# Joining an MLP's inner norm factor to its last norm, low parts on VectorE around it, and four split weight tiles kept between the token halves

## The chip, the core and the metric

The kernel runs on one core of a Trainium2 chip. The metric is the device time of one execution, in microseconds (us); less is better. The engines are called as in the profile: PE (TensorE's matmuls), PEld (its weight loads), DVE (VectorE), ACT (ScalarE), POOL (GpSimd) and SP (SyncE, which issues loads here).

## The reference

The whole program is a two-block network over 512 tokens of width 1024. The first block (a state-space mixer, a short convolution and an expert layer) is not touched. The part that matters is the end of the second block, after its two attentions `out_a` and `out_b`:

```python
def rmsnorm_2(x, g):
    y = x * rsqrt(mean(x * x, axis=-1) + EPS)      # EPS = 1e-6
    return y * g

merged = sigmoid(g_a) * (out_a @ w_o_a) + sigmoid(g_b) * (out_b @ w_o_b)
x = x + rmsnorm_2(merged @ w_out, post_norm_mix)
h2 = rmsnorm_2(x, pre_norm_mlp)
y = square(relu(h2 @ w_up)) @ w_down               # 1024 -> 4096 -> 1024
x = x + rmsnorm_2(y, post_norm_mlp)
```

All weights and activations are float32. The factor of the inner norm (`rsqrt(mean(x*x) + EPS)`, one number per token) is positive, so it can be taken through `relu` and through the matmuls, and out of the square as its own square.

## The kernel before

Everything is kept transposed: model width on the 128 partitions in 8 slices, tokens along the free dimension. A float32 product is made of three: each operand is split into a rounded high part and the low part that is left (`split`, L173 to 180: ScalarE rounds, another engine subtracts), and PE multiplies high by high, high by low and low by high (`mm3`, L201). One block is the product for one 128-wide slice of outputs: 8 slices of input times 3, that is 24 matmuls, over 512 tokens or over a half of 256.

Weights come through `weights` (L182): SyncE loads 512 KB into `wr` (3 buffers), ScalarE rounds it into `wh` (L176), and GpSimd, or VectorE where the call says so, subtracts it into `wl` (L177); `wh` and `wl` have 3 buffers each. In the stages below GpSimd makes the low parts, except for every second block of the last down-projection.

`block2` ends with these stages, in this order:

- The gated projections, 8 blocks of 512 tokens: products `po`, times the gates (`g`, L1223), added (`m`, L1225, on GpSimd), split into `m2h`, `m2l`.
- The output projection (`out_block`, L1233), run for tokens 0 to 255 and then for 256 to 511, 8 blocks (`psw`) each. ScalarE copies the result to `y` (the tile `oab`) and squares it, VectorE adds the squares up (`sqadd`, L1350).
- For each half `chain` (L1249): `norm` (L1239) takes row sums of the squares on PE (`ssqr`), a reciprocal root by 12 small VectorE instructions (`rsqrt`, names r3), a broadcast by PE (`prr`); then for each slice the scaling (L1255), the addition into the residual (L1256), the split into `d2h`, `d2l` with the MLP's gain (L179, L180), the square and its addition. At its end a second `norm` (r4) makes the factor of the inner norm, which ScalarE copies into `rb` (L1262).
- The up-projection, 4 quarters of 8 blocks (`up`, L1291; products `psup`). In the first quarter the first `nh` = 5 blocks run by halves, so that the first half's products cover the second half's chain, and the steps of the chains stand between the blocks. After each block `up_act` (L1285) takes `max(psup, 0) * rb` on VectorE, its square on ScalarE, and the split into `fh`, `fl`.
- The down-projection (`down`, L1314; products `psdn`), one quarter of the inner width behind each quarter of the up-projection; results are added up in `y`. The last quarter runs by halves again, with a norm (r5) and the final scaling and addition (`finish`, L1323) for each half. `finish` works on VectorE, with five of its eight additions on GpSimd.

Each engine works through its instructions in order. A list scheduler puts them in order from the program; `keep_in_program_order` holds the row sums and broadcasts at their place among PE's instructions. The order of the first quarter of the up-projection is written out by hand:

```python
for n, (j, tk) in enumerate([(j, tk) for tk in halves for j in range(nh)]
                            + [(j, slice(0, S)) for j in range(nh, 8)]):
    ready.append((f, j, tk, up_mm(q, j, n, tk)))
    if n == 0:
        next(first, None)
    if n in (0, 1, nh, nh + 1):
        next(second, None)
```

## Time and profile before

| | |
|---|---|
| median of 3 runs | 2861.68 us (2855.43 to 2865.1) |
| the profiled execution, its own time | 2858.98 us |
| its span, first to last instruction | 2857.1 us |
| granted TensorE clock over the span | 0.987 |
| PE busy | 2767.0 us, 97% |
| DVE / ACT / POOL busy | 1948.2 / 1095.3 / 854.9 us |

The page of the profile gives the busy sums for the whole span. The stages described above lie in its last 510 us, and times of events count from the span's start. Busy time of PE counts an instruction from start to modelled end, and consecutive matmuls overlap, so a block's duration is read from the distance of like events in neighbouring blocks or from a merged row of the chain of waits. The duration in a DVE row likewise overlaps a little with the next instruction; the distance of two starts is what it costs.

### The profile page before, as it was taken

The page shows a single profiled execution, that of the slowest core. Times are in us where ns is not written, and L with a number is a line of the kernel's source. Part 1 is how long each engine was busy: PE and PEld are TensorE (multiplying, and loading weights), DVE is VectorE, ACT ScalarE, POOL GpSimd, SP SyncE. Part 2 cuts the span into 40 slices and gives each one's busy share as a digit, 9 for nine tenths or more (in the row PEclk, how much of TensorE's full clock was granted, in tenths as well). Part 3 has the DMA queues.
Part 4 walks back from the last instruction along what each step waited for, and adds up shares of the span by engine and source line. Part 5 has one row for each costly group of instructions (what it writes and reads, how often), then busy time and mean ns, then how long its engine had stood idle before and what let it go on. Part 6 is the DMA issues. An engine that isn't in the chain of part 4 may idle for free. (4 is left out here: it accounts for less than half of the span.)

```text
span 2857.1 us, 40181 instructions
## 1 busy us (share of the span) xinstructions
PE 2767.0 (97%) x15502; PEld 2387.7 (84%) x15502; DVE 1948.2 (68%) x3687; ACT 1095.3 (38%) x1742; POOL 854.9 (30%) x464
## 2 busy tenths in 40 slices
PE   8999999999999999899999999999999999799997
PEld 7988888877888999899999998887787778788887
DVE  8433777775279997857887777888975655841236
ACT  4222433343233444444333333333345553443232
POOL 4444444444542002100322221222200016444443
PEclk9999999999999999999999999999999999899998
DMA  3222122223332668689988888999822225332223
GB/s 132 89 96 96 60 67 67 67 67 122 123 124 82 223 201 276 219 275 303 376 309 320 310 309 331 384 377 370 315 91 94 78 74 168 106 104 96 96 96 119
DMA packets 174736, 515.21 MB, mean 180 GB/s; under 512 B 14160, under 2 KB 75600, under 8 KB 158032
## 3 DMA queue, kind: packets, MB, share of 16 engines
q1 hardware_dynamic: 91328, 330.75, 33.8%
q0 software_dynamic: 18432, 134.23, 12.1%
q10 hardware_dynamic: 64784, 47.67, 5.2%
q8 instruction: 122, 2.00, 0.3%
q14 instruction: 70, 0.57, 0.1%
HBM read 462.97 MB, written 49.09 MB: 179 GB/s over the span
## 5 line engine op out<-in xcount | busy, mean ns | idle before, releaser
L176 ACT ACTIVATE wh<-wr 128x1024 fp32r<-128x1024 f32 (+1 forms) x525 | 553.8, 1055 | 1113.3 <-issue 239.5
L177 POOL TENSOR_TENSOR wl<-wr,wh 128x1024 fp32r<-128x1024 f32 x229 | 552.3, 2413 | 962.5 <-ACT wh L176 952.1
L851 POOL DMA_INDIRECT gb<-puv,idx x128 | 209.3, 1635 | 931.8 <-DVE gacc L860 779.3
L177 DVE TENSOR_TENSOR wl<-wr,wh 128x1024 fp32r<-128x1024 f32 (+1 forms) x296 | 359.6, 1216 | 153.7 <-ACT wh L176 150.3
L201 PE MATMUL psu<-u2h,wh 128*128 128x384 f32 x1024 | 348.9, 341 | 0.0
L201 PE MATMUL psu<-u2h,wl 128*128 128x384 f32 x1024 | 346.1, 338 | 1.4 <-DVE wl L177 1.4
L201 PE MATMUL psu<-u2l,wh 128*128 128x384 f32 x1024 | 345.1, 337 | 0.0
L201 PE MATMUL mmt<-uh,wh 128*128 128x264 f32 (+2 forms) x1016 | 328.8, 324 | 4.2 <-ACT uh L176 3.5
L201 PE MATMUL mmt<-ul,wh 128*128 128x264 f32 (+2 forms) x1016 | 329.0, 324 | 0.0
L201 PE MATMUL mmt<-uh,wl 128*128 128x264 f32 (+2 forms) x1016 | 326.5, 321 | 0.0
L1043 PE MATMUL acc<-wh,ch 128*128 128x512 f32 x768 | 305.9, 398 | 3.9 <-ACT ch L176 2.4
L1043 PE MATMUL acc<-wl,ch 128*128 128x512 f32 x768 | 305.7, 398 | 1.3 <-DVE wl L177 1.3
L1043 PE MATMUL acc<-wh,cl 128*128 128x512 f32 x768 | 305.4, 398 | 0.1
L201 PEld LDWEIGHTS mmt<-ul,wh 128*128 128x128 f32 x1016 | 192.3, 189 | 21.5 <-issue 10.0
L201 PEld LDWEIGHTS mmt<-uh,wh 128*128 128x128 f32 x1016 | 192.3, 189 | 19.0 <-ACT uh L176 3.7
L201 PEld LDWEIGHTS mmt<-uh,wl 128*128 128x128 f32 x1016 | 192.3, 189 | 15.0 <-issue 3.3
L201 PEld LDWEIGHTS psu<-u2h,wh 128*128 128x128 f32 x1024 | 194.7, 190 | 2.2
L201 PEld LDWEIGHTS psu<-u2l,wh 128*128 128x128 f32 x1024 | 194.3, 190 | 2.0
L201 PEld LDWEIGHTS psu<-u2h,wl 128*128 128x128 f32 x1024 | 193.7, 189 | 2.4 <-DVE wl L177 2.4
L1043 PEld LDWEIGHTS acc<-wl,ch 128*128 128x128 f32 x768 | 145.2, 189 | 38.5 <-DVE wl L177 3.5
L1043 PEld LDWEIGHTS acc<-wh,ch 128*128 128x128 f32 x768 | 145.3, 189 | 37.5 <-ACT ch L176 2.7
L1043 PEld LDWEIGHTS acc<-wh,cl 128*128 128x128 f32 x768 | 145.1, 189 | 33.1 <-DVE cl L177 0.4
(498 smaller groups left out, 5558.1 us busy)
## 6 DMA issues: line engine op xcount, KB each, us to landing
wr<-pu SPq DMA_DIRECT2D x128, 512.0 KB, 5.6
wr<-pv SPq DMA_DIRECT2D x128, 512.0 KB, 6.3
mg<-md SPq DMA_DIRECT2D x34, 768.0 KB, 10.4
md<-stg ACTq DMA_DIRECT2D x24, 1024.0 KB, 7.5
wr<-w_dn SPq DMA_DIRECT2D x40, 512.0 KB, 3.6
wr<-w_up SPq DMA_DIRECT2D x37, 512.0 KB, 3.7
actd<-at ACTq DMA_DIRECT2D x79, 192.0 KB, 3.8
ag<-actd SPq DMA_DIRECT2D x19, 768.0 KB, 6.8
```

The lines of the kernel that those rows point to most:

```text
L176: nc.scalar.activation(h, src, AF.Copy)
L177: (eng or nc.vector).tensor_tensor(l, src, h.bitcast(F32), op=OP.subtract)
L201: self.nc.tensor.matmul(ps, a[:, k], b, start=first and n == 0, stop=last and n == tot - 1)
L851: keep(nc.gpsimd.indirect_dma_start(out=rows[k][:NG], out_offset=None, in_=self.A["puv"], in_offset=bass.IndirectOffsetOnAxis(ap=idx[:NG, ...
L1043: self.nc.tensor.matmul(self.accs[i], a[:, t], b[:, d], start=e == self.e1 and n == 0, stop=e == self.e1 - 1 and n == 2)
```

## The change

The inner norm's factor is no longer applied between the up- and the down-projection. The MLP runs on the residual with only the gain, `relu` and square included, so its result is too large by the inverse square of the factor, per token; the last norm divides by its own root mean square anyway, and only its epsilon has to be corrected: with `e = mean(x*x) + EPS`, the last norm uses `EPS * e * e` in place of `EPS` (`eps4`). The sums for it are made during the second quarter's down-projection (`inner_norm`). `up_act` squares as `relu(psup)` on ScalarE and then `max(psup, 0)` times that on VectorE. In the first up-projection `nh` is 7.

Low parts of weights are made on VectorE in the gated projections, the output projection, the first quarter of the up-projection and the last of the down-projection, but on GpSimd for the blocks where `low` says so (a counter that leaves 1 when divided by 3). The addition of the gated projections goes to VectorE too.

`kept_weights` splits a weight tile into a slice of a pair of large tiles instead of the rotating `wh`, `wl`. In the output projection, the first quarter of the up-projection and the last of the down-projection, four of the blocks keep their split weights so from the first half to the second, which runs these four blocks first and loads nothing for them.

```diff
@@ -184,6 +184,15 @@
         self.nc.sync.dma_start(wr, ap)
         return self.wsplit(wr, kn, eng)
 
+    def kept_weights(self, ap, room, i, eng=None):
+        w = [t[:, 2 * i:2 * i + 2].rearrange("p a (b o) -> p (a b) o", o=128) for t in room]
+        if ap is not None:
+            wr = self.wraw.tile([128, 8, 128], F32, tag="wr", name="wr")
+            self.nc.sync.dma_start(wr, ap)
+            self.split(w[0], w[1], wr, eng=eng or self.nc.gpsimd)
+        return w
     def wsplit(self, wr, kn=8, eng=None):
         wh = self.whl.tile([128, kn, 128], F32R, tag="wh", name="wh")
         wl = self.whl.tile([128, kn, 128], F32R, tag="wl", name="wl")
@@ -222,12 +231,15 @@
             if keep and t == 0:
                 self.tc.keep_in_program_order(m)
 
-    def rsqrt(self, p, src, scale, tag, eps=True):
+    def rsqrt(self, p, src, scale, tag, eps=None):
 
         v = self.nc.vector
         shp = list(src.shape)
         x, y, a = [p.tile(shp, F32, tag=tag + n, name=tag + n) for n in ("x", "y", "a")]
-        v.tensor_scalar(x, src, scale, EPS, op0=OP.mult, op1=OP.add)
+        if eps is None:
+            v.tensor_scalar(x, src, scale, EPS, op0=OP.mult, op1=OP.add)
+        else:
+            v.scalar_tensor_tensor(x, src, scale, eps, op0=OP.mult, op1=OP.add)
         self.newton(x, y, a)
         return y
 
@@ -1215,14 +1227,14 @@
         for d in range(8):
             g2 = p.tile([128, 2, S], F32, name="g2")
             nc.sync.dma_start(g2, self.gd[d::8].rearrange("g p s -> p g s"))
-            wh, wl = self.weights(A["w_oab"][d])
+            wh, wl = self.weights(A["w_oab"][d], eng=v)
             for i, pp in ((0, self.mm2), (1, sp)):
                 ps = pp.tile([128, S], F32, tag=("mm", "s")[i], name="po%d" % i)
                 ks = slice(4 * i, 4 * i + 4)
                 self.mm3(ps, (wh[:, ks], wl[:, ks]), [(o[0][:, k], o[1][:, k]) for k in range(4 * i, 4 * i + 4)])
                 v.tensor_tensor(g2[:, i], g2[:, i], ps, op=OP.mult)
             t = p.tile([128, S], F32, name="m2")
-            nc.gpsimd.tensor_tensor(t, g2[:, 0], g2[:, 1], op=OP.add)
+            v.tensor_tensor(t, g2[:, 0], g2[:, 1], op=OP.add)
             self.split(m[0][:, d], m[1][:, d], t)
 
         y = oab
@@ -1230,17 +1242,24 @@
         H = S // 2
         halves = [slice(0, H), slice(H, S)]
 
+        low = lambda n: nc.gpsimd if n % 3 == 1 else v
         def out_block(d, tk):
             ps = (sp if d % 2 else self.mm2).tile([128, S], F32, tag="s" if d % 2 else "mm", name="psw2")[:, :H]
-            self.mm3_real(ps, self.weights(A["w_out"][d]), m, off=tk.start, n=H)
+            if d < 4:
+                w = self.weights(A["w_out"][d], eng=low(tk.start // H * d))
+            else:
+                w = self.kept_weights(None if tk.start else A["w_out"][d], kept, d - 4, v)
+            self.mm3_real(ps, w, m, off=tk.start, n=H)
             act.activation(y[:, d, tk], ps, AF.Copy)
-            self.sqadd(cn, y[:, d, tk], d, v, tk.start)
-
-        def norm(pool, tag, name, key):
+            self.sqadd(cn, y[:, d, tk], (d + 4) % 8 if tk.start else d, v, tk.start)
+        def norm(pool, tag, name, key, eps=None):
 
             ssq = pool.tile([128, 512], F32, tag=tag, name="ssq" + name)
             self.rowsum(ssq, self.sums[key], True, True, 2, keep=True)
-            r = self.rsqrt(cn, ssq[:, :2], 1.0 / D, name)
+            r = self.rsqrt(cn, ssq[:, :2], 1.0 / D, name, eps)
             yield
             pr = pool.tile([128, 512], F32, tag=tag, name="pr" + name)[:, :H]
             self.bcast(pr, r, 2, keep=True)
@@ -1255,66 +1274,82 @@
                 v.scalar_tensor_tensor(y[:, d, tk], y[:, d, tk], par("post_mix", d), pr, op0=OP.mult, op1=OP.mult)
                 v.tensor_tensor(x, x, y[:, d, tk], op=OP.add)
                 self.split(self.d[0][:, d, tk], self.d[1][:, d, tk], x, gain=par("pre_mlp", d))
-                self.sqadd(cn, x, d, v, "x")
             yield
-            n = norm(op_, "o", "r4", "x")
-            yield next(n)
-            act.activation(self.rb[:, tk], next(n), AF.Copy)
-
+        kept = [op2.tile([128, 8, S], F32R, name=n) for n in ("oh2", "ol2")]
         for d in range(8):
             out_block(d, halves[0])
         steps = chain(halves[0])
-        for d in range(8):
+        for n, d in enumerate((4, 5, 6, 7, 0, 1, 2, 3)):
             out_block(d, halves[1])
-            if d < 2:
+            if n < 2:
                 next(steps, None)
-        steps = (steps, chain(halves[1]))
+        steps = chain(halves[1])
         self.dump("x2", self.res)
         self.close("mgt2", "mg2", "ohl")
 
+        eps4 = cn.tile([128, 4], F32, name="eps4")
+        def inner_norm():
+            for d in range(8):
+                self.sqadd(p, self.res[:, d], d, v, "x")
+                yield
+            ssq = op_.tile([128, 512], F32, tag="o", name="ssqr4")
+            self.rowsum(ssq, self.sums["x"], True, True, 4, keep=True)
+            v.tensor_scalar(eps4, ssq[:, :4], 1.0 / D, EPS, op0=OP.mult, op1=OP.add)
+            v.scalar_tensor_tensor(eps4, eps4, EPS, eps4, op0=OP.mult, op1=OP.mult)
+            yield
         fp = self.open("ff", 2)
+        room = lambda: [fp.tile([128, 8, S], F32R, name=n) for n in ("fh", "fl")]
         p = self.open("fft", 2)
         fs = {}
+        nh = 7
+        kept = room()
 
         def up_mm(q, j, n, tk):
             ps = (sp if n % 2 and q == 0 else self.mm2).tile([128, S], F32, tag="s" if n % 2 and q == 0 else "mm",
                                                              name="psup")[:, tk]
-            self.mm3_real(ps, self.weights(A["w_up"][q * 8 + j]), self.d, off=tk.start, n=tk.stop - tk.start)
+            if q == 0 and nh - 4 <= j < nh:
+                w = self.kept_weights(None if tk.start else A["w_up"][j], kept, j - nh + 4, low(n))
+            else:
+                w = self.weights(A["w_up"][q * 8 + j], eng=None if q else low(n))
+            self.mm3_real(ps, w, self.d, off=tk.start, n=tk.stop - tk.start)
             return ps
 
         def up_act(f, j, tk, ps):
             r = p.tile([128, S], F32, name="r")[:, tk]
-            v.scalar_tensor_tensor(r, ps, 0.0, self.rb[:, tk], op0=OP.max, op1=OP.mult)
-            act.activation(r, r, AF.Square)
+            act.activation(r, ps, AF.Relu)
+            v.scalar_tensor_tensor(r, ps, 0.0, r, op0=OP.max, op1=OP.mult)
             self.split(f[0][:, j, tk], f[1][:, j, tk], r)
 
         def up(q):
-            f = fs[q] = [fp.tile([128, 8, S], F32R, name=n) for n in ("fh", "fl")]
+            f = fs[q] = room()
             if q:
                 for j in range(8):
                     up_act(f, j, slice(0, S), up_mm(q, j, j, slice(0, S)))
                 return
 
-            first, second = steps
-            next(first)
-            nh = 5
-            ready = []
-            for n, (j, tk) in enumerate([(j, tk) for tk in halves for j in range(nh)]
+            for n, (j, tk) in enumerate([(j, halves[0]) for j in range(nh)]
+                                        + [(j, halves[1]) for j in (*range(nh - 4, nh), *range(nh - 4))]
                                         + [(j, slice(0, S)) for j in range(nh, 8)]):
-                ready.append((f, j, tk, up_mm(q, j, n, tk)))
-                if n == 0:
-                    next(first, None)
-                if n in (0, 1, nh, nh + 1):
-                    next(second, None)
-                if n != nh:
-                    for x in ready:
-                        up_act(*x)
-                    ready = []
+                up_act(f, j, tk, up_mm(q, j, n, tk))
+                if n in (0, 1):
+                    next(steps, None)
 
         def down(f, q, d, tk):
             ps = sp.tile([128, S], F32, tag="s", name="psdn")[:, tk]
-            self.mm3_real(ps, self.weights(A["w_dn"][q, d], eng=v if q == 3 and d % 2 else None), f,
-                          off=tk.start, n=tk.stop - tk.start)
+            if q < 3 or d < 4:
+                w = self.weights(A["w_dn"][q, d], eng=v if q == 3 else None)
+            else:
+                w = self.kept_weights(None if tk.start else A["w_dn"][q, d], kept, d - 4, v)
+            self.mm3_real(ps, w, f, off=tk.start, n=tk.stop - tk.start)
             if q == 0:
                 act.activation(y[:, d, tk], ps, AF.Copy)
             else:
@@ -1328,22 +1363,29 @@
                 if d % 2:
                     nc.sync.dma_start(self.O[:, d - 1:d + 1, tk], y[:, d - 1:d + 1, tk])
 
+        inner = inner_norm()
         up(0)
         for q in range(3):
             up(q + 1)
             f = fs.pop(q)
             for d in range(8):
                 down(f, q, d, slice(0, S))
+                if q == 1:
+                    next(inner, None)
+            if q == 1:
+                next(inner)
         n, last = None, None
+        kept = room()
         for tk in halves:
-            for d in range(8):
+            for i in range(8):
+                d = (i + 4) % 8 if last else i
                 down(fs[3], 3, d, tk)
-                self.sqadd(cn, y[:, d, tk], d, v, tk.start)
-                if last and d == 0:
+                self.sqadd(cn, y[:, d, tk], i, v, tk.start)
+                if last and i == 0:
                     next(n)
-                if last and d == 1:
+                if last and i == 1:
                     finish(last, next(n))
-            n, last = norm(tp, "t", "r5", tk.start), tk
+            n, last = norm(tp, "t", "r5", tk.start, eps4[:, tk.start // 128:tk.start // 128 + 2]), tk
         next(n)
         finish(last, next(n))
```

## Rows read from the trace of the kernel before

**Rows 1.** The page, part 1: busy us, share of the span, instructions.

```profile
PE 2767.0 (97%) x15502; PEld 2387.7 (84%) x15502; DVE 1948.2 (68%) x3687; ACT 1095.3 (38%) x1742; POOL 854.9 (30%) x464
```

**Rows 2.** Five stretches: us; PE, PEld, DVE, ACT, POOL busy; clock; DMA.

```profile
2347.89:2453.50 105.61, 96.07 (x588) 86.09 (x586) 64.21 (x79) 44.24 (x75) 67.05 (x32) 0.97 0.49 157
2453.50:2525.55 72.05, 55.21 (x329) 50.42 (x329) 52.43 (x96) 32.69 (x62) 34.63 (x15) 0.83 0.33 107
2657.47:2702.27 44.80, 44.80 (x194) 36.07 (x193) 7.31 (x9) 9.65 (x11) 19.18 (x8) 1.00 0.30 96
2745.80:2842.97 97.17, 93.20 (x583) 83.73 (x581) 46.50 (x69) 29.83 (x39) 37.28 (x19) 0.98 0.36 117
2842.97:2857.10 14.13, 1.32 (x6) 0.89 (x6) 8.08 (x25) 0.42 (x1) 3.63 (x5) 0.57 0.22 74
```

**Rows 3.** PE's waits from 2347.89 to 2525.55: us, times, longest.

```profile
PE prr L246 <- DVE r4y L241: 11.1, 2, 8.1
PE psup L201 <- ACT d2h L179: 3.0, 2, 2.6
PE psw L201 <- ACT m2h L176: 2.7, 1, 2.7
PE psup L201 <- DVE d2l L180: 2.5, 2, 1.8
...
PE psw L201 <- DVE m2l L177: 1.7, 1, 1.7
...
PE po L201 <- DVE g L1223: 0.7, 1, 0.7
```

**Rows 4.** PE's waits from 2745.80 to 2857.10.

```profile
PE psdn L201 <- DVE oab L1321: 2.9, 1, 2.9
```

**Rows 5.** DVE in order of time: start us, us, instruction.

```profile
2442.55 0.86 DVE L1255 SCALAR_TENSOR_TENSOR oab<-oab,pt,prr 128x256 f32<-128x256 f32 x2
2443.34 0.41 DVE L1256 TENSOR_TENSOR res<-res,oab 128x256 f32<-128x256 f32 x1
2443.67 0.47 DVE L180 SCALAR_TENSOR_TENSOR d2l<-res,pt,d2h 128x256 fp32r<-128x256 f32 x1
2444.07 0.41 DVE L1358 TENSOR_TENSOR sq<-sq 128x256 f32<-128x256 f32 x1
...
2446.70 2.43 DVE L1256 TENSOR_TENSOR res<-res,oab 128x256 f32<-128x256 f32 x1
```

**Rows 6.** POOL's groups, 2347.89 to 2525.55: busy us, mean ns.

```profile
L177 POOL TENSOR_TENSOR wl<-wr,wh 128x1024 fp32r<-128x1024 f32 x38 | 92.1, 2431 | 88.8 <-ACT wh L176 88.7
```

**Rows 7.** The chain of waits: start us, us, what.

```profile
2401.12 13.19 PE psw L201 x96
...
2429.55 0.17 DVE r3a L239
...
2569.15 44.79 PE psdn L201 x192
2613.94 43.53 PE psup L201 x192
...
2829.83 13.15 PE psdn L201 x96
```

**Rows 8.** DVE in order of time, last down-projection.

```profile
2793.48 0.42 DVE L1321 TENSOR_TENSOR oab<-oab,psdn 128x256 f32<-128x256 f32 x1 [2.17 <-PE psdn L201]
...
2796.33 0.42 DVE L1321 TENSOR_TENSOR oab<-oab,psdn 128x256 f32<-128x256 f32 x1 [0.60 <-PE psdn L201]
...
2800.34 1.21 DVE L177 TENSOR_TENSOR wl<-wr,wh 128x1024 fp32r<-128x1024 f32 x1
2801.47 0.41 DVE L1358 TENSOR_TENSOR sq<-sq 128x256 f32<-128x256 f32 x1
```

**Rows 9.** One stretch, only instructions on d2h: PE, PEld, DVE, ACT.

```profile
2474.00:2480.00 6.00, 6.00 (x34) 5.17 (x34) 3.28 (x3) 1.50 (x3) 1.00 0.25 87
```

**Rows 10.** ACT in order of time, one weight tile's rounding.

```profile
2475.99 1.04 ACT L176 ACTIVATE wh<-wr 128x1024 fp32r<-128x1024 f32 x1
```

## The prediction

> **What bounds the kernel now.** I read the engine line of the page first [rows 1]. PE is busy for 97% of the span, so outside a few holes only fewer or faster matmuls could help, and the change removes none: whatever it gains must come out of holes. Then I cut the stages that the diff touches into stretches [rows 2]: A, the gated projections and the output projection; B, the first quarter of the MLP's up-projection; one ordinary down-projection for comparison; C, the last down-projections; and the tail after the last matmul. The comparison stretch has PE busy all 44.80 us at granted clock 1.00. A lacks 9.5 us of PE work, B lacks 16.8 us, C lacks 4.0 us, and the clock is below 1.00 in all three, at 0.83 in B. So each hole is paid for twice: while PE stands still, and afterwards at the lower of its two levels (1.2 instead of 2.4 GHz).
>
> The size of that second payment: a half block (24 matmuls over 256 tokens) takes 2.85 us at full clock, the distance between the two evictions at 2793.48 and 2796.33 [rows 8]. After the holes at the start of the output projection four half blocks took 13.19 us, and after the hole in the last stage 13.15 us [rows 7], where four times 2.85 is 11.4: about 1.8 us lost behind a hole.
>
> The waits say which work comes late. In A and B [rows 3] the largest is the broadcast of the inner norm's factor (r4), 11.1 us in two pieces; then the rounded input of the up-projection's second half (d2h and d2l, 5.5 us), then and the end of the merged input (m2h, m2l, 4.4 us). In C it is an eviction behind the final scaling, 2.9 us [rows 4]. What makes VectorE late there is seen in its own order of time [rows 5]: an addition into the residual takes 0.33 us (2443.34 to the next start), and the same addition at 2446.70 takes 2.43, which is the length of a low part on POOL (2431 ns, 38 of them in A and B, [rows 6]). VectorE stands until POOL's instruction is over.
>
> **The change part by part.** I compare each stretch with what its matmuls need without a hole. A full block is 43.53/8 = 5.44 us in an up-projection and 44.79/8 = 5.60 in a down-projection [rows 7], which I also take for a gated projection (512 columns too). The two PE steps of a norm, row sums and broadcast, are estimated at 1.0 us together: two of the one and one of the other cost what the holes around them leave, and the busy shares do not resolve more.
>
> *The inner norm leaves the front.* Both r4 chains (row sums, 12 small VectorE steps, broadcast) go from B: 11.1 us of waits and 2.0 us of PE steps. VectorE also loses 16 additions of squares there. The eight squares and additions that come instead, over 512 tokens, fall into the second down-projection, where VectorE is busy 7.31 and ScalarE 9.65 of 44.80 us [rows 2]; eight additions of 0.66 (twice the width of the 0.33), or 2.4 each behind POOL, still fit under PE. If that cover were gone they would cost 5.3 us. Not hidden are the four row-sum matmuls, some 0.6 us, which wait for the last addition: between 0 and 3 us (one eviction plus one blocked addition); I take 0.5, because the residual is ready long before. The corrected epsilon is one small instruction at each end norm where there was one already: nothing.
>
> *Relu on ScalarE, then a product on VectorE.* The same number of instructions as the product and the square now, in the other order; the accumulator is held by two steps instead of one. A half block's accumulators rotate over four buffers and a full block's over two, so there are at least 5.4 us for about 1.5. Nothing, while ScalarE has idle time; and the matmuls no longer wait through full buffers for the factor.
>
> *Low parts to VectorE.* One costs 1.13 us there (2800.34 to 2801.47, [rows 8]) against 2.43 on POOL. In A and B four stay on POOL (output block 1 of the second half, and n = 1, 4 and 13 in the up-projection); in C none. The sum for VectorE over output projection and first up-projection: 16 additions of squares at 0.33, 16 slices of the residual chain at 0.39 + 0.33 + 0.40 [rows 5], some 19 low parts at 1.13, 15 evictions and splits at 0.42 + 0.33 [rows 5, 8], 22 small steps at 0.17 [rows 7]: 60 us against 93 us of PE. The last merged slice no longer queues behind a low part on POOL, nor its m2l behind the next one; its addition, rounding and low part, three steps of some 0.65, run beside the 21 matmuls that do not need it (2.5 us), so some 0.5 us of the 4.4 us hole stay.
>
> The Trainium skill, "Perfetto Trace Analysis", section "Optimizing Scalar/DVE Operations", would move work the other way: a saturated VectorE may be relieved onto GpSimd, though the port that they share may undo it. VectorE is busy 52.43 of 72.05 us in B [rows 2], so by that rule the low parts would cost and not gain where VectorE sets the pace; by the locked additions of the row they gain. The row is of this kernel, and I go by it; the rule's way is the first rival.
>
> *Kept weights.* Four of eight blocks' split weights serve both halves, at three places. Twelve loads, twelve roundings on ScalarE and twelve low parts go. Loads never bounded PE here, so by itself this is worth nothing; it frees VectorE in the first half of each second half, where the norm chain runs, and pays for the low parts above.
>
> *Seven halved blocks instead of five.* Two more blocks run as two halves: 2 x (2 x 2.85 - 5.44) = 0.5 us more PE time. They give the chain of the second half 7 x 2.85 = 20 us of cover instead of 14. From its broadcast, after two blocks, to its need there are 5 x 2.85 + 2.5 = 16.7 us. VectorE must do 8 x 1.12 = 9.0 of chain, five evictions and splits (3.7), three low parts (3.4) and stand behind one of POOL's (2.0): 18.1. It comes out about 1.4 us short, plus 1.8 for the clock.
>
> The sum by stretch:
> - A: 8 x 5.60 + 16 x 2.85 + 1.0 = 91.4, now 105.61. I leave 2.5 (0.7 for a gate load that stays late, [rows 3], 0.5 at the merge, 1.3 for the first norm). Gain 11.7; between 4 (only the merge's hole) and 14.2.
> - B: 14 x 2.85 + 5.44 + 1.0 = 46.3, now 72.05. I leave 5.0 (3.2 as above, 0.8 for the broadcast, 1.0 at its start). Gain 20.7; between 13 (r4 alone) and 25.7.
> - C: 8 x 5.60 + 16 x 2.85 + 1.0 = 91.4, now 97.17. The final scaling still stands in front of an eviction, on VectorE and POOL together; I leave 1.5 of the 2.9 and no clock loss. Gain 4.3; between 1 and 5.8.
> - Inner norm in the second down-projection: minus 1.1 (0.6 to 3.6).
> - Tail: 14.13 us [rows 2], the same instructions: nothing.
>
> Together 35.6 us, off the profiled execution's 2858.98 us: 2823.4. The median of the runs lies 2.7 us above that execution, so I forecast 2826.
>
> **The rivals.** First, VectorE becomes the bound (the rule above). For it: 18.1 us of work against 16.7, and its queue is in order, so low parts fetched ahead for the next weights may stand in front of the chain (two more at 1.13 and a second of POOL's at 2.0), the first chain may also end some 2.5 us late, with another 1.8 of clock, and in C the final scaling holds an eviction as now (3.2 more). That is 2.3 + 2.0 + 2.5 + 1.8 + 3.2 = 11.8 more: 2838. Against it: 60 of 93 us on the whole.
>
> Second, and slower: the four kept weights are slices of one tile. If a write to a slice waited for the readers of the others, no kept block could be prepared while its predecessor runs. Each would cost one rounding (1.04, [rows 10]) and one low part (1.13) with PE idle, behind other work of 2 us at most, and 1.8 for the clock: 4.1 to 5.9. There are 3 x 3 such blocks: 37 to 53 us, so 2863 to 2879. It decides from 4 us a block. Against it: from 2474 to 2480 ScalarE writes three slices of the second half of d2h while PE, busy all 6.00 us, multiplies by its first half [rows 9].
>
> Third, the holes only move: the r4 wait covered the second half's r3 chain, which was late too (5.5 us of waits on d2h and d2l behind it). If seven blocks do not cover it, B keeps that and one clock loss: about 7 us less gain than forecast, some 2833, inside the first rival's lower end.
>
> **How the numbers follow.** Forecast, 2818 to 2832: 0.62. First and third rival, 2832 to 2848: 0.27. Second rival, slower: 0.05. The last 0.06 goes half to a better end (nothing left in B: 2815) and half to no change. The range 2817 to 2842 leaves out the second rival, the upper end of the first and part of the better end. Of a difference over 0.3% (8.6 us, about what this kernel's measurement can tell): faster 0.92, same 0.03, slower 0.05.
>
> **What would show it.** Right: no r4 broadcast in front of the up-projection; PE idle under 5 us in A and under 5 in B, granted clock above 0.95 there; additions on VectorE near 0.4 us except beside the four low parts left on POOL; the first up-projection some 50 us long. Wrong: waits of the second half's matmuls on d2h or d2l of several us, evictions late in C behind the scaling, or kept weights' rounding that waits for PE's previous block.

## The result, and the profile after

The changed kernel takes 2811.78 us (median of 4 runs, 2808.72 to 2815.92) against 2858.55 us (4 runs, 2847.71 to 2865.1): ratio 0.9828, 95% interval 0.9812 to 0.9844. It is faster, as forecast, but by more: 2811.78 lies 14 us under the forecast of 2826 and 5 us under the low end of the range. The profiled execution took 2809.85 us with a span of 2808.1.

The page of the changed kernel, part 1, answers to [rows 1]. PE has 18 us less busy time, POOL 115 us less.

```profile
PE 2748.7 (98%) x15546; PEld 2375.7 (85%) x15546; DVE 1912.5 (68%) x3701; ACT 1082.9 (39%) x1726; POOL 739.6 (26%) x415
```

The same five stretches of the changed kernel, with the columns of [rows 2]:

```profile
2341.86:2432.43 90.57, 90.31 (x583) 81.89 (x582) 61.59 (x102) 40.62 (x67) 3.85 (x2) 1.00 0.52 166
2432.43:2483.30 50.87, 48.07 (x369) 46.75 (x368) 41.57 (x80) 29.26 (x58) 10.89 (x5) 0.97 0.38 119
2614.31:2658.44 44.13, 44.13 (x196) 36.22 (x194) 6.63 (x9) 9.75 (x11) 19.22 (x8) 1.00 0.30 99
2702.72:2793.91 91.19, 90.46 (x583) 81.99 (x581) 39.35 (x73) 25.92 (x35) 18.34 (x11) 1.00 0.31 102
2793.91:2808.10 14.19, 1.24 (x6) 0.81 (x6) 8.08 (x25) 0.42 (x1) 3.63 (x5) 0.62 0.22 74
```

Row by row against [rows 2]: A is 15.0 us shorter and lacks 0.3 us of PE work instead of 9.5; B is 21.2 shorter and lacks 2.8 instead of 16.8; C is 6.0 shorter and lacks 0.7 instead of 4.0; the tail is the same. The third row is an ordinary down-projection, the comparison stretch, and it too got shorter: 44.13 us against 44.80. (The third and fourth windows here begin at the first down-projection matmul, those of [rows 2] 0.16 us later, at the end of the last up-projection one. Cut alike, the comparison stretch is 0.83 us shorter and C 6.1.) The stretch from the end of B to the start of C took 220.25 us before (2525.55 to 2745.80) and takes 219.42 now, 0.8 less, although it now holds the inner norm. The granted clock rose from 0.97 to 1.00 in A, from 0.83 to 0.97 in B and from 0.98 to 1.00 in C, as holes went. So the gain in A, B and C is of two kinds. PE's holes there shrank by 26.6 us (9.3 + 14.0 + 3.2). What the lower clock takes away, estimated from the rows as one minus the granted clock times the stretch, fell from some 17 us (3.2 + 12.2 + 1.9) to 1.5.

PE's waits in A and B of the changed kernel, against eleven kinds before, the main ones in [rows 3]:

```profile
PE prr L258 <- DVE r3y L253: 2.0, 1, 2.0
PE psup L210 <- ACT r L1328: 0.8, 1, 0.8
PE po L210 <- DVE g L1235: 0.3, 1, 0.3
```

and in C and the tail (the first two belong to the tail's norm), against [rows 4]:

```profile
PE prr L258 <- DVE r5y L253: 2.5, 1, 2.5
PE ssqr L229 <- DVE sq L1400: 1.6, 1, 1.6
PE psdn L210 <- DVE oab L1356: 0.7, 1, 0.7
```

The waits for d2h, d2l, m2h and m2l are gone, r4 with them. The chain of waits (start, us, what) shows how long blocks take when nothing holds them:

```profile
2353.29 33.21 PE po L210 x144
2386.51 25.94 PE psw L210 x216
...
2526.94 43.96 PE psdn L210 x192
2570.90 43.57 PE psup L210 x192
...
2782.78 11.14 PE psdn L210 x96
```

The last four half blocks took 13.15 us in [rows 7], behind a hole, and take 11.14 here, so the second payment for C's hole, at most 2.0 us, is no longer made. Nine half blocks of the output projection run in 25.94 us, 2.88 each, where four took 13.19.

A, B, the stretch between, C and the tail together give 43.0 us, but the two spans differ by 49.0. The other 6.0 us lie ahead of A. Of these, 1.7 are between the first query product of the attentions and A; they were in no term of the forecast. The other 4.3 are ahead of that product, where the change touches nothing: in the profiles of the variants below the same start comes anywhere from 2154.7 (the changed kernel) to 2162.9 us. So the change itself gives 44.7 us in this pair, and the remaining 4.3 is the spread of the earlier stages. The ratio's interval is 44.6 to 53.7 us (0.0156 and 0.0188 of 2858.55), and 44.7 stands at its lower end.

### The profile page after: what moved, and what is told of

The parts are those of the page before. It is cut to its first block, busy times and chain, and to the rows that moved or that the text cites. A ratio compares the mean times of both kernels' runs of the same rounds, so it can differ in the third digit from the quotient of the medians.

```text
span 2808.1 us, 40116 instructions
## 1 busy us (share of the span) xinstructions
PE 2748.7 (98%) x15546; PEld 2375.7 (85%) x15546; DVE 1912.5 (68%) x3701; ACT 1082.9 (39%) x1726; POOL 739.6 (26%) x415
## 4 chain that ended last, share of the span: by engine, by line
PE 54%; DVE 11%; issue 5%; DMA 5%; ACT 1%; POOL 1%; ACTq 0%; SPq 0%; DVEq 0%; POOLq 0%
PE acc L1055 13%; PE psu L210 11%; PE mmt L210 6%; PE psup L210 6%; PE psdn L210 6%; PE ps L210 5%; DMA wr<-pv 4%; DVE wl L177 2%; PE psw L210 2%; PE po L210 1%; POOL gb L863 1%; DVE gb L890 1%; PE psml L1564 1%; ACT wh L176 1%; PE oml L1584 1%
## 5 line engine op out<-in xcount | busy, mean ns | idle before, releaser
L176 ACT ACTIVATE wh<-wr 128x1024 fp32r<-128x1024 f32 (+1 forms) x503 | 530.6, 1055 | 1083.6 <-issue 228.5
L177 POOL TENSOR_TENSOR wl<-wr,wh 128x1024 fp32r<-128x1024 f32 x187 | 450.0, 2406 | 991.4 <-ACT wh L176 981.1
L177 DVE TENSOR_TENSOR wl<-wr,wh 128x1024 fp32r<-128x1024 f32 (+1 forms) x316 | 383.9, 1215 | 163.3 <-ACT wh L176 162.6
L863 POOL DMA_INDIRECT gb<-puv,idx x128 | 203.3, 1588 | 934.8 <-DVE gacc L872 782.3
```

Source lines behind the costliest of these rows:

```text
L176: nc.scalar.activation(h, src, AF.Copy)
L177: (eng or nc.vector).tensor_tensor(l, src, h.bitcast(F32), op=OP.subtract)
L863: keep(nc.gpsimd.indirect_dma_start(out=rows[k][:NG], out_offset=None, in_=self.A["puv"], in_offset=bass.IndirectOffsetOnAxis(ap=idx[:NG, ...
```

## The experiments

The theory at first was that each part fills holes of its own: low parts A and C, the joined norm B; the kept weights are worth nothing alone and pay for the low parts' time on VectorE. The rivals were that one part does nearly all of it, and that VectorE becomes the bound where the kept weights are missing.

The table cuts every profile at the starts of the first matmul of a kind (query product, gated projection, up-projection, down-projection), so that the spread of the earlier stages stays out of it. "Ahead" is the attention part before A, "B + quarter" also holds the up-projection's second quarter, "mid" reaches from the first down-projection to the last up-projection's end. All in us, worked out from starts in the traces.

| kernel | ahead | A | B + quarter | mid | C | tail | total | against before |
|---|---|---|---|---|---|---|---|---|
| before | 188.9 | 105.6 | 115.5 | 176.8 | 97.2 | 14.1 | 698.1 | |
| changed | 187.2 | 90.6 | 94.4 | 176.1 | 91.0 | 14.2 | 653.4 | -44.7 |
| low_only | 187.2 | 98.7 | 106.7 | 176.8 | 94.9 | 14.1 | 678.6 | -19.5 |
| inner_only | 189.0 | 105.7 | 101.5 | 176.1 | 97.2 | 14.2 | 683.7 | -14.4 |
| kept_only | 188.9 | 98.0 | 108.8 | 176.8 | 98.2 | 14.3 | 685.0 | -13.1 |
| no_low | 188.9 | 97.4 | 108.7 | 176.1 | 94.4 | 14.1 | 679.7 | -18.4 |
| no_inner | 187.2 | 91.8 | 105.4 | 176.8 | 92.0 | 13.9 | 667.1 | -31.0 |
| no_kept | 187.2 | 99.5 | 100.8 | 176.1 | 91.9 | 13.9 | 669.4 | -28.7 |
| nh5 | 187.2 | 90.7 | 99.3 | 176.1 | 90.5 | 14.3 | 658.2 | -39.9 |
| all_dve | 187.2 | 90.6 | 94.8 | 176.1 | 91.3 | 14.2 | 654.2 | -43.9 |
| oab_pool | 188.9 | 91.4 | 93.1 | 176.1 | 90.5 | 14.1 | 654.2 | -43.9 |
| pad | 188.9 | 106.8 | 115.9 | 177.2 | 97.3 | 13.8 | 700.0 | +1.9 |
| place | 188.9 | 106.9 | 118.6 | 175.2 | 94.7 | 14.2 | 698.6 | +0.5 |

**The kernel before, again** (no edit): the measurement's own spread.

> The unchanged kernel once more. In the two traces at hand the gated projections begin at 2347.9 us before and at 2341.9 us after, though nearly all instructions ahead of them are the same. If those 6.0 us are what one execution differs from the next by, this trace starts them anywhere within some 6 us of 2348, and the three stretches from there on repeat within 1 us (A 105.6, B 72.1, C 97.2). If they belong to the change, this trace starts them at 2348 within 1 us. Time: same as before, within 0.3%.

2858.87 us, ratio 1.0013 [0.9998, 1.0027]; ten runs lie between 2854.93 and 2867.45. Its total in the table's terms is 698.5, no stage more than 0.1 us off: of one kernel, stages repeat far more finely than whole runs. Its gated projections start at 2347.3, within 1 us of the first trace, which by the expectation would give the 6.0 us to the change. But three of the kernels below that differ from the changed one in a single line (nh5, all_dve, oab_pool) start the first query product at 2159.1 to 2162.9, no earlier than the kernel before (2159.0); so the 4.3 us ahead of it are the execution's and not the change's.

**One part alone.** The low parts on VectorE:

```diff
-            wh, wl = self.weights(A["w_oab"][d])
+            wh, wl = self.weights(A["w_oab"][d], eng=v)
-            nc.gpsimd.tensor_tensor(t, g2[:, 0], g2[:, 1], op=OP.add)
+            v.tensor_tensor(t, g2[:, 0], g2[:, 1], op=OP.add)
+        low = lambda n: nc.gpsimd if n % 3 == 1 else v
...   (w_out: eng=low(tk.start // H * d); w_up: eng=None if q else low(n))
-   self.weights(A["w_dn"][q, d], eng=v if q == 3 and d % 2 else None)
+   self.weights(A["w_dn"][q, d], eng=v if q == 3 else None)
```

> Only the low parts and the merge's addition go to VectorE; inner norm, five halved blocks and no kept weights as before. Theory one (VectorE stands behind POOL's low parts, and each hole is paid again by the clock): A falls to 92 to 94 us (gain 12 to 14), C to 92 to 93, B loses its blocked small steps and additions, some 8 to 12 of its 25 us of holes; 24 to 30 us faster in all. Rival (VectorE is the bound, low parts there cost): A and B gain under 3 us each, or lose.

The joined norm, with `nh` = 5:

```diff
-            v.scalar_tensor_tensor(r, ps, 0.0, self.rb[:, tk], op0=OP.max, op1=OP.mult)
-            act.activation(r, r, AF.Square)
+            act.activation(r, ps, AF.Relu)
+            v.scalar_tensor_tensor(r, ps, 0.0, r, op0=OP.max, op1=OP.mult)
...   (no r4 in chain; eps4, inner_norm and the end norm's epsilon as in the change)
```

> Only the inner norm is joined to the last one, with Relu on ScalarE; low parts where they were, five halved blocks, no kept weights. Theory one: B loses the r4 waits and broadcasts, 11.1 + 2.0 us and two pieces of slow clock, 13 to 17 us; A and C stay within 1 us. Rival (the r4 wait only covered the second half's r3 chain, which is late behind POOL): B gains under 8 us, and waits on d2h and d2l of the second half grow from 5.5 to over 10 us.

The kept weights, with low parts where they were before, r4 as before and `nh` = 5:

```diff
+            if d < 4:
+                w = self.weights(A["w_out"][d], eng=None)
+            else:
+                w = self.kept_weights(None if tk.start else A["w_out"][d], kept, d - 4, nc.gpsimd)
...   (the same for w_up and w_dn, and the second half's order of blocks)
```

> Only the four kept weights at three places, their low parts made on GpSimd as the others, five halved blocks, inner norm in its old place. Twelve loads, roundings and low parts fewer. Theory one: loads did not bound PE, but POOL has 12 locks of 2.4 us fewer, eight of them in A and B: 2 to 7 us faster. Rival: nothing (within 2 us); or the slower one of the prediction (a write to one slice waits for readers of the others): 30 us slower or more.

Measured: low parts 0.9924 [0.9904, 0.9944] (2835.47 us), joined norm 0.9952 [0.9934, 0.9971] (2845.14 us), kept weights 0.9956 [0.9939, 0.9973] (2845.23 us). All three are faster by themselves, the kept weights too. In the table they come to 19.5 + 14.4 + 13.1 = 47.0 us, near the 44.7 of all three, so no part does nearly everything. The pairs below show that the parts are not independent for all that.

Not all of it came as expected. The low parts gave A 6.9 us instead of 12 to 14, because PE waits 4.6 us there for low parts and roundings of weights (wl 3.3, wh 1.3). The kept weights gave 13.1 instead of 2 to 7.

Where the kept weights' 13.1 us come from is told by the stages: 7.6 in A and 6.7 in B and the quarter behind it, less 1.0 that C loses. First, what locks the r4 chain in the kernel before, VectorE and POOL in order of time:

```profile
2455.74 7.15 POOL L177 TENSOR_TENSOR wl<-wr,wh 128x1024 fp32r<-128x1024 f32 x3 [1.76 <-ACT wh L176]
2456.42 1.97 DVE L1358 TENSOR_TENSOR sq<-sq 128x256 f32<-128x256 f32 x1 [1.09 <-ACT sq L1354]
...
2458.49 2.13 DVE L236 TENSOR_SCALAR r4a<-r4x 128x2 int32<-128x2 int32 x1
2460.66 2.26 DVE L237 TENSOR_SCALAR r4y<-r4a 128x2 int32<-128x2 int32 x1
```

Three low parts run back to back on POOL, and three VectorE steps, an addition of squares and two small steps of the chain, each stand until one of them is over. With 6.4 us together they are most of the 8.1 us wait in [rows 3]. The same two small steps of the kernel with kept weights alone are:

```profile
2447.97 0.17 DVE L245 TENSOR_SCALAR r4a<-r4x 128x2 int32<-128x2 int32 x1
2448.17 0.17 DVE L246 TENSOR_SCALAR r4y<-r4a 128x2 int32<-128x2 int32 x1
```

POOL, in order of time, shows why, and that the reason is not the same everywhere:

```profile
2438.79 2.67 POOL L177 TENSOR_TENSOR wl<-wr,wh 128x1024 fp32r<-128x1024 f32 x1 [18.15 <-ACT wh L176]
...
2453.85 9.41 POOL L177 TENSOR_TENSOR fl<-wr,fh 128x1024 fp32r<-128x1024 f32 x4 [7.90 <-DVE r3a L249]
...
2496.29 2.39 POOL L177 TENSOR_TENSOR wl<-wr,wh 128x1024 fp32r<-128x1024 f32 x1 [21.72 <-ACT wh L176]
```

In the second half of the output projection POOL stands idle for 18.15 us, and in the second half of the up-projection for 21.72: there the low parts are gone, because the split weights are still in SBUF, and the first half's r3 chain and the second half's r4 chain beside them run free. Beside the first half's r4 chain nothing is gone. The up-projection's weights are split for the first time there, only later, from 2453.85, when that chain is over; PE then waits for them. Among PE's waits in that kernel's A and B are:

```profile
PE psup L210 <- ACT fh L176: 2.6, 1, 2.6
PE prr L255 <- DVE r4y L250: 1.3, 1, 1.3
...
PE psup L210 <- POOL fl L177: 0.9, 1, 0.9
```

The r4 waits fall from 11.1 us to 1.3, but 3.5 us on a kept tile (fh, fl) are new. In A the waits for a low part on POOL, for the squares and for r3y, 4.0 us in the kernel before, are gone, and only 4.1 for m2h are left.

A step on 2 elements of each partition costs 0.17 us free and 2.26 us beside a low part. The Trainium skill, "SBUF — State Buffer", section "Who interferes with whom", lists tensor_scalar among the VectorE operations that can take the pair of ports shared with GpSimd, whoever is first holding it for the whole instruction; these rows agree, and show that even the shortest instruction pays it in full.

**One part taken out of the change.** Without the low parts on VectorE (`low` always GpSimd, merge addition on GpSimd, the last down-projection's low parts shared as before):

```diff
-        low = lambda n: nc.gpsimd if n % 3 == 1 else v
+        low = lambda n: nc.gpsimd
...   (w_oab without eng=v; kept w_out blocks on nc.gpsimd; w_dn by d % 2)
```

> The changed kernel with the low parts and the merge's addition on GpSimd as before. If parts add up: 19 to 23 us above the changed kernel, 2831 to 2835, and the gated projections start 1.5 us later behind a hole in the last attention (low part on GpSimd at some 2314, VectorE's product behind it). If the kept weights and the inner norm alone take enough locks away: under 10 us.

Without the joined norm (the kernel before plus low parts, kept weights and `nh` = 7), against the change:

```diff
+                self.sqadd(cn, x, d, v, "x")
+            n = norm(op_, "o", "r4", "x")
+            yield next(n)
+            act.activation(self.rb[:, tk], next(n), AF.Copy)
...   (up_act, the end norm and the order of steps as before)
```

> The changed kernel with the inner norm's factor in its old place (both r4 chains in the first up-projection), seven halved blocks, kept weights and low parts as changed. If parts add up: 10 to 14 us above the changed kernel, 2821 to 2826, nearly all of it in B. If seven halved blocks cover the r4 chain now that VectorE is not locked: under 4 us. The down-projections run at 44.95 us a quarter again if their speed hangs on where the tiles lie (eps4 gone), at 44.1 otherwise.

Without kept weights:

```diff
-                w = self.kept_weights(None if tk.start else A["w_out"][d], kept, d - 4, v)
+                w = self.weights(A["w_out"][d], eng=v)
...   (w_up: self.weights(A["w_up"][j], eng=low(n)); w_dn: eng=v)
```

> The changed kernel without kept weights: the four blocks load and split their weights again in the second half, on the engines that made them in the first. Alone the kept weights gave 11.4 us. If the three parts take away different holes (they gave 21.2, 11.5 and 11.4 alone, 44.1 in sum, against 44.8 together), this lies 9 to 13 us above the changed kernel, 2821 to 2825. If, as the prediction had it, they only free VectorE of low parts that PE covers anyway, it lies within 3 us. If VectorE is at its limit in the first up-projection without them, over 18 us.

Measured: without low parts 0.994 [0.9916, 0.9964] (2840.95 us), without the joined norm 0.9881 [0.9856, 0.9907] (2828.25 us), without kept weights 0.9883 [0.986, 0.9907] (2827.57 us), all against 2861.22 of the kernel before. By the table they lose 26.3, 13.7 and 16.0 of the 44.7 us. The low parts are worth most, 19.5 alone and 26.3 in company, where 19 to 23 had been expected.

Each of these kernels is also a pair of parts, and the pairs differ. Low parts and kept weights give 31.0 us, nearly their sum of 32.6. Low parts and joined norm give 28.7 of 33.9. Joined norm and kept weights give only 18.4 of 27.5. In B with its quarter the joined norm gives 14.0 us alone and nothing beside the kept weights (108.7 against 108.8, with seven halved blocks against five). The trace without low parts on VectorE says why:

```profile
PE psup L210 <- DVE r L1329: 6.0, 1, 6.0
PE prr L258 <- DVE r3y L253: 5.1, 1, 5.1
```

The r4 waits are gone, and the second half's r3 chain and an eviction behind it are late in their place. Beside POOL's low parts from 2472.65 to 2480.02 three VectorE steps of that chain take 2.0, 2.5 and 2.5 us each. That is the forecast's third rival, holes that only move, and with the low parts moved to VectorE 2.0 us of it are left, at r3y in the changed kernel.

The waits of A and B without kept weights show the forecast's first rival, VectorE as the bound, at work:

```profile
PE psup L210 <- DVE r L1327: 3.4, 1, 3.4
PE psw L210 <- DVE wl L177: 3.2, 1, 3.2
PE psup L210 <- ACT d2h L179: 3.1, 1, 3.1
PE psw L210 <- ACT wh L176: 3.0, 1, 3.0
```

and so do those with the low parts alone:

```profile
PE psup L201 <- DVE r L1289: 6.7, 2, 5.7
PE psw L201 <- DVE wl L177: 3.3, 1, 3.3
```

PE waits for low parts (wl) and for evictions (r) on VectorE: its queue is in order, and both stand behind the norm chain. With kept weights both are gone from A and B of the changed kernel, and A falls from 99.5 to 90.6 us. Only the waits for wl belong to the moved low parts alone. An eviction was 6.0 us late above with the low parts on POOL, and without the joined norm, with kept weights, it is

```profile
PE psup L210 <- DVE r L1310: 6.2, 1, 6.2
```

so the moved low parts are not the only cause of that lateness. The rule on which the first rival stood (the Trainium skill, "Perfetto Trace Analysis", section "Optimizing Scalar/DVE Operations") speaks of relieving a saturated VectorE; here low parts moved onto VectorE gave a ratio of 0.9924 even by themselves, though the 3.3 us of waits for wl show that some of them did come late there.

**Seven or five halved blocks:**

```diff
-        nh = 7
+        nh = 5
```

> The changed kernel with five halved blocks in the first up-projection instead of seven (kept are blocks 1 to 4). The second half's chain took 12.7 us from its broadcast to its last d2l; three blocks after the broadcast cover 3 x 2.85 + 2.5 = 11 us, so a hole of 2 to 3 us with 1.8 of clock behind it, less the 0.5 us that two halved blocks cost: 3 to 5 us slower than the changed kernel, 2815 to 2817. Rival (seven are not needed once VectorE is not locked): within 1 us, or 0.5 us faster.

0.9858 [0.9841, 0.9874], 2819.36 us. The stage table has it 4.8 us behind the change, nearly all in B (99.3 against 94.4). The expected shortage of cover is the smaller part of it: PE waits 1.5 us for d2h and d2l, and 3.2 us for the first kept weights (fh, fl).

**No low part left on POOL in A and B:**

```diff
-        low = lambda n: nc.gpsimd if n % 3 == 1 else v
+        low = lambda n: v
```

> The changed kernel with every low part of these stages on VectorE, none left on GpSimd. In the changed kernel's trace the broadcast of the second half's norm comes 2.0 us late, and VectorE stands 2.3 us in one of that norm's small steps behind a low part on GpSimd (2439.04), 2.1 us in an addition of squares behind another (2430.99). If those locks are what is left, B loses the 2.0 us hole and about 1.3 us of slow clock: 2 to 4 us faster than the changed kernel, 2808 to 2810. Rival (VectorE is near its limit there, four more low parts of 1.13 us fall into its fullest stretch): holes of 1 to 4 us on d2h or d2l, 0 to 5 us slower than the changed kernel.

0.9832 [0.9815, 0.985], 2814.41 us: no difference from the change that can be measured, where 2 to 4 us less were expected. The 2.0 us hole that is left in B of the changed kernel is one small step behind one low part on POOL:

```profile
2439.04 2.59 POOL L177 TENSOR_TENSOR fl<-wr,fh 128x1024 fp32r<-128x1024 f32 x1 [5.65 <-ACT fh L176]
2439.33 2.32 DVE L252 SCALAR_TENSOR_TENSOR r3a<-r3a,r3x 128x2 f32<-128x2 f32 x1
```

With all low parts on VectorE it is gone, and another comes in A and B, an eviction that is late on VectorE:

```profile
PE psup L210 <- DVE r L1329: 3.8, 1, 3.8
```

The hole only moved. B + quarter is 94.8 us against 94.4.

**The gated projections' low parts back on POOL**, to find the 1.7 us ahead of A:

```diff
-            wh, wl = self.weights(A["w_oab"][d], eng=v)
+            wh, wl = self.weights(A["w_oab"][d])
```

> The changed kernel with only the gated projections' low parts on GpSimd again (the merge's addition stays on VectorE). If the first of them, at some 2310 us, is what made PE wait 1.4 us in the last attention (VectorE's gate behind GpSimd, ScalarE's queue behind the gate's store, PE behind ScalarE's copy), the 1.4 us come back ahead of the gated projections; A gets back 2 to 5 us of its 14.9. In sum 4 to 8 us slower than the changed kernel, 2816 to 2820. Rival (the hole ahead of A has another cause): nothing ahead of A, 0 to 4 us in it.

0.9845 [0.9823, 0.9866], 2815.76 us. "Ahead" is back at 188.9 us. A loses only 0.8 us of the 2 to 5 that were expected, and B gains 1.3: its holes are no smaller than the changed kernel's (2.0 us at r3y, 0.9 and 0.4 at r), but the granted clock stays at 1.00 there, against 0.97. The cause of what changes ahead of A is a step that nobody would look for there; POOL, VectorE and ScalarE of the kernel before, during the last attention:

```profile
2314.41 3.32 POOL L177 TENSOR_TENSOR wl<-wr,wh 128x1024 fp32r<-128x1024 f32 x1 [262.95 <-ACT wh L176]
2315.41 2.61 DVE L254 TENSOR_SCALAR gt<-gt 128x512 f32<-128x512 f32 x1
...
2318.05 0.33 ACTq L1203 DMA_DIRECT2D gd<-gt  x1
2318.42 1.08 ACT L1498 ACTIVATE PT<-ptsw 128x512 f32<-128x512 f32 x2 [4.15 <-DVE gt L254]
```

The first low part of the gated projections is made early, on POOL, which had been idle for 263 us. A gate on VectorE stands until it is over, the store of that gate in ScalarE's queue waits for the gate, the copy behind the store (PT) waits with it, and PE waits for the copy. ScalarE stands for 4.15 us ahead of that copy (2.03 in the changed kernel, where the copy is released by PE). PE's wait there, in the kernel before:

```profile
PE ptsw L1496 <- ACT PT L1498: 1.4, 1, 1.4
```

In the changed kernel the low part is on VectorE, in order with the gate, and the gate takes its 0.42 us:

```profile
2311.09 0.42 DVE L266 TENSOR_SCALAR gt<-gt 128x512 f32<-128x512 f32 x1
```

**The place of operands in SBUF.** The comparison stretch was faster after the change though its instructions are the same ones. Two kernels change no work of the matmuls, only the small tiles of the pool `cn`, and with them where later tiles lie. The first adds a tile of 128 x 4 and a memset of it; the second has that too and lets r4 use the tiles of r3, which takes three small ones away, so that the count is that of the changed kernel:

```diff
+        pad = cn.tile([128, 4], F32, name="pad")
+        v.memset(pad, 0.0)
...   (the second kernel also has this)
-            n = norm(op_, "o", "r4", "x")
+            n = norm(op_, "o", "r3", "x")
```

> The kernel before with one unused tile of 128 x 4 numbers in the pool in front of the operands, nothing else. In the changed kernel and in the one with the inner norm joined a down-projection of 8 full blocks takes 44.13 us and the last six gated projections 33.22, in the others 44.95 and 33.70, with the same instructions. If the place of the operands in SBUF makes that difference, this trace shows 44.1 and 33.2. If the values or the order of the norm make it, 44.95 and 33.70.

> The kernel before with its operands moved in SBUF as the joined inner norm moves them: r4's three small tiles share r3's, one unused tile of the same size is added. One pad alone gave 45.13 us for 8 full down-projection blocks instead of 44.95. If the place decides, 44.13 here, and 33.2 for the last six gated projections; if the joined norm does it in another way, 44.9 to 45.2 and 33.7.

One execution each (2863.19 and 2859.83 us), read for block durations only. The chain of waits of the first, one down-projection of 8 blocks (the up-projection behind it takes 43.53 us):

```profile
2573.27 44.98 PE psdn L201 x192
```

and of the second, a down- and an up-projection:

```profile
2574.16 43.96 PE psdn L201 x192
2618.12 43.57 PE psup L201 x192
```

Against 44.79 and 43.53 in [rows 7]. (The expectations cut 0.17 us later and so speak of 44.13 and 44.95.) The first kernel met neither of its expectations, being slower; the second met the one on place. The last six gated projections, from start to start, follow suit: 33.54 us before, 33.05 in the second kernel and in the changed one. The same 192 matmuls take 43.96, 44.79 or 44.98 us as small tiles elsewhere come and go, while the up-projection stays. All variants with the joined norm have 43.96; of those without it, all but these two have 44.79. The second kernel has none of the joined norm's arithmetic, so the layout alone makes the 0.83 us, and the joined norm's part in them is an accident of its tiles. Why a place is slower was not settled: no run separates which operand's place it is.

The same kernel is a warning on small differences between stages. Its total is that of the kernel before (+0.5), but B and its quarter are 3.1 us longer and C 2.5 shorter, with holes of the same size (16.8 and 16.8 us in the one, 4.1 and 4.0 in the other). What differs is the granted clock, here in the second kernel:

```profile
2749.22:2844.05 94.83, 90.65 (x583) 81.95 (x581) 46.48 (x70) 29.96 (x39) 37.41 (x19) 1.00 0.37 120
2455.35:2573.99 118.64, 101.87 (x519) 89.70 (x520) 73.78 (x112) 50.16 (x85) 53.67 (x23) 0.87 0.30 100
```

In the kernel before it was 0.98 in C and 0.90 in B with its quarter. In this one C's holes were followed by no lower clock at all, and part of its 2.5 us is the place of operands.

## Why the prediction was right, and where it fell short

**Right.** The direction, the reading that PE is bound outside holes, and that a hole is paid twice: every stretch that lost its holes got its clock back. The tail was forecast at nothing, and gave nothing. B was forecast at 20.7 us and gave 21.2, but in part by luck: the hole of 1.4 us in front of the second half's matmuls did not come, nor the 1.0 at the start, and in their place the broadcast came 2.0 us late instead of 0.8, behind one locked step, and the relu on ScalarE, put at nothing, 0.8. PE's idle time stayed under 5 us in A and B with the clock above 0.95, and the first up-projection lasts 50.87 us where some 50 was forecast. Seven halved blocks were needed. The first rival is real where a part is missing: without kept weights PE waits 3.2 us for a low part on VectorE, and with all low parts on VectorE 3.8 for an eviction. The second, slower one fell: in the changed kernel kept blocks run without a wait of their own, and with kept weights alone the waits for them are 3.5 us in all, where it needed 4 for each of nine blocks. The third did not happen in the changed kernel; it did in the one without low parts on VectorE.

**Short, by terms.** The time came out under the whole range, and holes that went explain that only in part. By the prediction's own sum, with nothing left in A, B and C (2.5 + 5.0 + 1.5), the time is 2817, the low end of its range; its "nothing left in B: 2815" does not follow from it (2826 less 5.0 is 2821). So the floors were too high as well, and of two terms that turned out as gains one was put at a loss and one at nothing.

- A, forecast 11.7, measured 15.0, over the forecast's own upper bound of 14.2. The step that failed is "I leave 2.5": the norm's steps and the merge are covered, and 0.3 us of holes is left, which is 2.2 of the miss. The remaining 1.1 is the floor of 91.4 itself, too high: six gated blocks take 33.21, 5.54 each where I used 5.60, and the sixteen half blocks with the norm's two PE steps take 46.1 where I had 46.6. The 5.60 was right for other layouts: with the low parts alone, eight gated blocks in the chain of waits take

```profile
2344.02 44.79 PE po L201 x192
```

- C, forecast 4.3, measured 6.0, over its upper bound of 5.8. I left 1.5; the eviction behind the final scaling now waits 0.7, and the eight full blocks in C are 0.8 shorter by their place.
- The inner norm in the second down-projection, forecast -1.1, measured +0.8 for the stretch between B and C. Two down-projections there are 0.83 shorter each, 1.7 in all, which leaves some 0.8 us for the norm's own cost. The additions were made long before, and no wait for them is left; the term was right in kind, and the place of operands, which the prediction did not know of, turned its sign.
- Ahead of A, forecast at nothing, measured 1.7. The stretches began at the gated projections, but their first low part runs earlier, beside the attention. The low parts moved; I followed where their matmuls are and not where they themselves run.

These misses are 3.3 (A) + 0.5 (B) + 1.7 (C) + 1.9 (inner norm) + 1.7 (ahead) = 9.1, from 35.6 to 44.7 us. The other 5 of the 14 us that the median lies below the forecast are the spread of the stages ahead: 4.4 by which the two profiled executions differ beyond the change, and 0.8 between the allowances from a profiled execution to its median (2.7 used, 1.9 now).

**Wrong in reasoning, although no term hung on it.** "Loads never bounded PE here, so by itself this is worth nothing": kept weights alone gave 13.1 us. The loads indeed did not bound PE (in the last 510 us of the kernel before no wait of PE or ScalarE is put down to one), but the low parts that go with them locked VectorE. The prediction had named that lock, and counted it for the low parts that move and not for those that vanish. Two of the change's three parts, low parts and kept weights, take the same kind of thing away: POOL instructions that run beside VectorE's chain. They take away different ones, so their gains nearly add up (31.0 of 32.6 us); it is the joined norm and the kept weights that overlap.

Two small slips in the working change nothing: two norms have 24 small steps and not 22, and the second rival's 4.1 to 5.9 us a block add up to 4.0 to 6.0.

## What to carry to other kernels

Where VectorE's steps are short and POOL's long, count what each POOL instruction does to the VectorE step beside it, and not only how long it lasts: removing or moving it can be worth more than its own time, in stretches where nothing else changed, ahead of the stage that it serves too. Removing work from a chain's neighbours, moving it onto the chain's engine and shortening the chain go together: here every pair of the three parts left an eviction on VectorE 3.4 to 6.2 us late in B, and with all three, as the change has them, PE waits for none there. A hole that goes may show the next one behind it, so a part's worth depends on which others are there. And a block duration that serves as a floor is measured in its own stage, since like matmuls differ by over 1% between stages and between layouts.

## What the runs showed of the hardware

- A VectorE step on 128 x 2 elements took 2.13 to 2.32 us beside a low part on POOL, and 0.17 free.
- 192 matmuls of one shape, at granted clock 1.00, took 43.96, 44.79 or 44.98 us, by where small tiles of another pool put the operands in SBUF.
- A store in ScalarE's queue was issued 0.03 us after the gate that it stores was ready (2318.05), and the copy behind it started only then (2318.42), after 4.15 us in which ScalarE stood; with the gate in time ScalarE stood 2.03 us there.
- After a hole of like size the four last half blocks of C took different times: 13.15 us in the kernel before (hole 2.9, granted clock 0.98 over C), 14.17 with the joined norm alone (hole 3.0, clock 0.96) and 11.69 in the second of the two kernels on place (hole 3.0, clock 1.00). So the second payment for a hole varies from case to case: 1.8 us was a fair size, and no constant.
